# Chaining a kernel's small TensorE products into rows: probabilities times values, and S5's

## The chip, the cores and the metric

One NeuronCore of a Trainium2 chip runs the whole program. The metric is device time in microseconds (us), the median of the runs. TensorE (PE in the views) does the matrix products, with weights loaded beside them (PEld); VectorE (DVE) and ScalarE (ACT) work on tiles of 128 partitions; SyncE (SP) issues most transfers. Products write to PSUM, which has eight banks here.

## What is computed

Two layers of a decoder trunk on one sequence of 1024 tokens and 1024 channels, all in float32. Each layer is two residual steps:

```python
# h <- LayerNorm(alpha*h + Mixer(h));  h <- LayerNorm(alpha*h + ConvFFN(h))
# Mixer: ONE combined input projection whose columns are
#   [attn q | attn k | attn v | rg-lru x | rg-lru gate | s5 u]
#   - dilated sliding-window attention (6 heads of 64, rotary q/k)
#   - RG-LRU branch (causal conv4 -> gated linear recurrence, times a GeLU gate)
#   - S5: complex diagonal state space, 16 groups of 16 channels, 64 states -> GELU -> GLU
#   each output RMS-normalised, concatenated, ONE output projection
# ConvFFN: up-projection (2 x 3072) -> causal depthwise conv (width 3) -> GeLU-gated product -> down
scores = einsum('bnqchd,bnkchd->bnchqk', q, k) / 8      # masked by a dilated window, three dilations
out    = einsum('bnchqk,bnkchd->bnqchd', exp(scores - logsumexp(scores)), v)
```

## The kernel before, in words

Channels lie on partitions and tokens on columns for the projections. Every dense product is made of float32 values split in a high and a low part of a faster type (fp32r): three products of 128x512 columns for one of full precision. The span falls into stages: projections and S5 (to 115 us), attention of layer 0 (115 to 300), output projection (to 437), up-projection of the FFN (437 to 901), down-projection (to 1135); layer 1 the same again, with its S5 in 1176 to 1245, its attention in 1245 to 1440 and the end at 2302.

**Attention** (`attend`, L1164) goes by three pairs of heads (p) in a layer. `score(i, h)` (L1168) makes the scores of 128 queries (block i) of head h, takes their minimum with a custom VectorE operation (P, nb in the views), the exponential on ScalarE, a reciprocal and a scaling on VectorE. `apply(Q)` (L1194) takes two blocks of queries: for each block j of 128 keys it transposes the probabilities of both heads on TensorE (pt), copies them out of PSUM (PT; VectorE for even j, ScalarE for odd), and multiplies them with the values (o). `pv` (L1199) issues that product for one j, one step after its copy: two calls, one for each head, each with 64 columns of values, so each writes 64 of the 128 partitions of o. While a pair of blocks is scored, the blocks before it go through `apply`; `fill` (L1705) puts dense products of later work in between.

**S5** works by chunks of tokens. `states` (L931) multiplies inputs U with WvT, in calls that write 64 partitions (vps). `outputs` (L960) adds for each of eight groups of columns and each half b the product of U with TK (128x128) and two products of the states x with CA, whose 64 rows are the lower or upper half (by b); all of one b and one half h of the columns is summed in one bank (yps).

**The order.** The program is not issued as it is written. Every call of an engine is recorded (`Traced`, L437), a `Graph` (L195) gives each a duration (`estimate`, L274) and each handover from one engine to another a delay (HANDOVER, L185), and a planner (`make_plan`, L481) finds an order for all calls, and places in a pool of 46 tiles, eight half tiles and eight PSUM banks: `sweep` (L305) lists calls forward and backward in time, `improve` (L419) repeats it, and of five cycles the order that is shortest by the planner's own model is kept. `issue` (L145) emits it; each engine then runs its instructions in that order and waits on semaphores for the others. All recorded calls therefore carry line L149 in the views, and are told apart by the tile that they write. A product for one j or one q is one call to the planner, placed wherever it fits.

Of the kernel before, what the change touches and what calls it, by code (L numbers as in the profile page):

```python
# [40 lines left out]
RESP = 1  # L41
HOOKS = ((0, 1, "outputs_in"), (0, 7, "glu"))
# [75 lines left out]

class NoSlot(Exception):
# [3 lines left out]
class Planner:  # L123
# [36 lines left out]
    def scheduled(self, tc):  # L160
        return [self.position[i.name] for block in tc.compile_state.ordered_instructions_by_block.values()
                for i in block if i.name in self.position]

    def place(self, order):
        use = {}
        for t, c in enumerate(order):
            _, args, kwargs = self.calls[c]
            for a in (*args, *kwargs.values()):
# [26 lines left out]
class Graph:  # L195
# [7 lines left out]
    def __init__(self, planner):  # L203
# [7 lines left out]
        for c, (f, args, kwargs) in enumerate(calls):  # L211
            self.engine.append(ENGINES[str(f.__self__.engine).split(".")[-1]])
# [61 lines left out]
    def estimate(self, c, name, outs, ins):  # L274
        e = self.engine[c]
        n = size(outs[0].ap[1:])
        if e == "PE":
# [4 lines left out]
            elif outs[0].shape[0] == 64 and n > 127:  # L282
                t = n * 1.55 / 2.4
            else:
                t = (2 * n + 8) / 2.4
        elif e == "SP":
            t, self.bytes[c] = 60, size(outs[0].ap) * 4
        else:
            n = max([n] + [size(a.ap[1:]) for a in ins])
            if e == "ACT":  # L290
                t = 205 + 0.83 * n + (150 if n == 1024 and outs[0].dtype == F32 else 0)
            elif e == "POOL":
                t = 200 + n
            elif name == "scalar_tensor_tensor" and len(outs[0].ap) > 2 and n == 1024:
                t = 2125
            else:
                a, b = VECTOR.get(name, (145, 1.044))
                t = a + b * n
        self.time[c] = round(t)
# [137 lines left out]
class Traced:  # L437
# [5 lines left out]
    def __getattr__(self, name):  # L443
        f = getattr(self.engine, name)
        return lambda *args, **kwargs: self.calls.append((f, args, kwargs))

# [53 lines left out]
def emit(tc, A, out, planner, trace):  # L500
    nc = tc.nc
    V, ACT, POOL, PE, SP = (Traced(e, planner.calls) for e in (nc.vector, nc.scalar, nc.gpsimd, nc.tensor, nc.sync))
    with ExitStack() as ctx:
# [397 lines left out]
        class S5:  # L901
# [29 lines left out]
            def states(self):  # L931
# [886 lines left out]
```

## Time and profile before

| | |
|---|---|
| median of the runs | 2303.13 us |
| lowest | 2301.6 us |
| profiled execution | 2303.53 us |
| its span (first to last instruction) | 2301.7 us |
| TensorE matmul busy | 2242.8 us (97%) |
| weight loads busy | 1811.4 us (79%) |
| VectorE busy | 2045.1 us (89%) |
| ScalarE busy | 1154.0 us (50%) |
| chain that ended last | PE 84%, DVE 10%, ACT 3%, DMA 2%, issue 1% |

A busy time is the union of an engine's instruction times; matmuls are pipelined, so a record of 0.39 us of a product can be followed by the next after 0.23 us, and what an instruction costs is the distance from start to start. In a timeline, records of one kind that follow each other are drawn together, with their count; a float32 call leaves two records, an fp32r call one. PEclk is the TensorE clock granted, as a share of full speed.

### The profile page before, as it was taken

The numbers are of one execution on the slowest core, as the hardware profiler recorded it, in microseconds if no ns is written. First come the engines' busy times: TensorE is split into PE (matmuls) and PEld (weight loads), VectorE is DVE, ScalarE is ACT, GpSimd is POOL, SyncE is SP. The second block draws the span as 40 slices with busy tenths as digits, with TensorE's granted clock in tenths as the row PEclk, the third lists the DMA queues.
The fourth block names the chain that finished last, engine by engine and source line by source line (L and its number), as shares of the span: only waits on it lengthen the run. The fifth ranks groups of instructions, "written<-read, shape, count | busy, mean of one in ns | idle before, by whom it ended". The sixth has DMA issues, their size and how long they took to land.

```text
span 2301.7 us, 28256 instructions
## 1 busy us (share of the span) xinstructions
PE 2242.8 (97%) x10520; PEld 1811.4 (79%) x10520; DVE 2045.1 (89%) x3357; ACT 1154.0 (50%) x1773; POOL 4.0 (0%) x8
## 2 busy tenths in 40 slices
PE   8999999999999999999998899999999999999996
PEld 6867778878888888888886677788888888788884
DVE  8888878898888989999995877888899899899999
ACT  4275673754444445444735457727455444454441
POOL 0000000000000000000000000000000000000000
PEclk9999999999999999999999899999999999999998
DMA  5321150222233435322333521401222244363312
GB/s 208 87 80 44 33 174 29 83 83 83 92 110 138 158 108 201 110 99 103 128 101 94 180 74 42 147 36 75 91 84 99 92 155 156 108 215 111 120 69 83
DMA packets 82169, 246.38 MB, mean 107 GB/s; under 512 B 12464, under 2 KB 20784, under 8 KB 82032
## 3 DMA queue, kind: packets, MB, share of 16 engines
q1 hardware_dynamic: 82032, 244.59, 31.4%
q8 instruction: 82, 1.34, 0.2%
q14 instruction: 55, 0.45, 0.1%
HBM read 176.26 MB, written 60.82 MB: 103 GB/s over the span
## 4 chain that ended last, share of the span: by engine, by line
PE 84%; DVE 10%; ACT 3%; DMA 2%; issue 1%; DVEq 0%; ACTq 0%; SPq 0%
PE uP_n L149 34%; PE dP_n L149 17%; PE o_n L149 3%; PE s_n L149 2%; PE pt_n L149 2%; DVE yf_n L149 1%; PE yps_n L149 1%; DVE cg_n L149 1%; DMA wu_n<-in_w_up_dram 1%; DVE daP_n L149 1%; PE ups00c_n L149 1%; DVE dbP_n L149 1%; PE gtps01c_n L149 1%; PE vps_01c_n L149 1%; DVE cv_n L149 1%
## 5 line engine op out<-in xcount | busy, mean ns | idle before, releaser
L149 PE MATMUL dP_n<-dbP_n,daP_n 128*128 128x512 f32 x2016 | 462.2, 391 | 12.6 <-DVE yf_n L149 11.8
L149 PEld LDWEIGHTS dP_n<-dbP_n,daP_n 128*128 128x128 f32 x2016 | 379.6, 189 | 92.5 <-issue 12.5
L149 ACT ACTIVATE dbP_n<-wr_n 128x512 fp32r<-128x512 f32 x168 | 102.8, 627 | 104.7 <-DVE wr_n L149 49.7
L149 ACT ACTIVATE wA_n<-wu_n 128x512 fp32r<-128x512 f32 x144 | 89.9, 628 | 122.4 <-PE uP_n L149 41.9
L149 ACT ACTIVATE wS_n<-wu_n 128x512 fp32r<-128x512 f32 x144 | 90.2, 630 | 111.5 <-DVE wu_n L149 41.3
L149 ACT ACTIVATE daP_n<-gr_n 128x512 fp32r<-128x512 f32 x144 | 89.5, 628 | 112.8 <-PE dP_n L149 48.2
L149 DVE SCALAR_TENSOR_TENSOR cg_n<-ga_n,small,cg_n 128x1023 f32<-128x1023 f32 x96 | 122.9, 1280 | 23.4 <-ACT cg_n L149 22.6
L149 DVE SCALAR_TENSOR_TENSOR cv_n<-va_n,small,cv_n 128x1023 f32<-128x1023 f32 x96 | 122.8, 1280 | 16.2 <-ACT cv_n L149 16.0
L149 DVE TENSOR_TENSOR yf_n<-yf_n,dP_n 128x512 f32<-128x512 f32 x192 | 127.9, 689 | 4.4 <-PE dP_n L149 2.4
L149 DVE TENSOR_TENSOR dbP_n<-wr_n,dbP_n 128x512 fp32r<-128x512 f32 x168 | 116.0, 694 | 0.3 <-ACT dbP_n L149 0.3
L149 DVE TENSOR_TENSOR daP_n<-gr_n,daP_n 128x512 fp32r<-128x512 f32 x144 | 99.8, 694 | 2.4 <-ACT daP_n L149 2.4
L149 DVE TENSOR_TENSOR wS_n<-wu_n,wS_n 128x512 fp32r<-128x512 f32 x144 | 98.2, 687 | 3.3 <-ACT wS_n L149 2.8
L149 DVE TENSOR_TENSOR wA_n<-wu_n,wA_n 128x512 fp32r<-128x512 f32 x144 | 97.8, 687 | 3.1 <-ACT wA_n L149 2.9
L149 ACT ACTIVATE cg_n<-ga_n,small 128x1024 f32<-128x1024 f32 x48 | 59.7, 1243 | 73.9 <-DVE ga_n L149 51.2
L149 PE MATMUL pt_n<-ident,P_n 128*128 128x128 f32 x432 | 74.3, 285 | 11.2 <-DVE P_n L149 10.1
L149 PEld LDWEIGHTS pt_n<-ident,P_n 128*128 128x128 f32 x432 | 53.4, 144 | 33.7 <-DVE P_n L149 11.6
L149 DVE CUSTOM_DVE_ANT_0 P_n<-s_n,mask_n 128x512 f32<-128x512 f32 (+3 forms) x96 | 55.4, 586 | 22.6 <-PE s_n L149 21.9
L149 ACT ACTIVATE cv_n<-va_n,small 128x1024 f32<-128x1024 f32 x48 | 59.4, 1238 | 24.7 <-DVE va_n L149 18.5
L149 PE MATMUL o_n<-PT_n,vt_n 128*64 128x256 f32 (+1 forms) x480 | 71.1, 375 | 0.0
L149 DVE TENSOR_TENSOR uu_n<-uP_n,p_n 128x512 f32<-128x512 f32 x96 | 65.9, 687 | 3.7 <-PE uP_n L149 3.4
L149 PE MATMUL uP_n<-T1T4h_n,wA_n 128*128 128x512 f32 x192 | 64.0, 394 | 2.1 <-DVE uu_n L149 2.1
L149 PE MATMUL uP_n<-T0T3h_n,wS_n 128*128 128x512 f32 x192 | 63.4, 391 | 2.3 <-DVE uu_n L149 2.3
(2279 smaller groups left out, 5974.7 us busy)
## 6 DMA issues: line engine op xcount, KB each, us to landing
wu_n<-in_w_up_dram SPq DMA_DIRECT2D x96, 512.0 KB, 3.5
gd<-cg_n SPq DMA_DIRECT2D x48, 512.0 KB, 2.9
gr_n<-gd SPq DMA_DIRECT2D x48, 512.0 KB, 4.4
wr_n<-in_w_down_dram SPq DMA_DIRECT2D x48, 512.0 KB, 5.1
yr_n<-hres SPq DMA_DIRECT2D x24, 512.0 KB, 3.8
hres<-yr_n SPq DMA_DIRECT2D x24, 512.0 KB, 3.2
hres<-y_n SPq DMA_DIRECT2D x16, 512.0 KB, 2.6
yf_n<-hres SPq DMA_DIRECT2D x16, 512.0 KB, 5.2
```

The source lines that it names most:

```text
L149: i = f(*args, **kwargs)
```

## The change

A context `PE.row()` collects the matmul calls made inside it into one `Row`. To the planner a row is one call, with 350 (TURN, in ns) added to the sum of its calls' estimates; when it is issued, its calls follow each other, each bound to the one before by a dependency without a semaphore. The first is bound in that way to the twelve TensorE instructions ahead of it (BARRIER), and an instruction that follows within twelve is bound to the last of the row. Three places use rows: the products of probabilities and values, now collected over several key blocks (RUNS: after block 2; 4; 3 and 6; 4 and 8, by Q); S5.states (eight calls in a row); and S5.outputs, where TK's products are split in two halves of 64 columns and put in one row of 16 calls, and CA's 16 in a second. The planner's costs are changed as well.

```diff
+RUNS = ((2,), (4,), (3, 6), (4, 8))
...
     def issue(self, tc):
-        last = {}
-        for n in self.order:
-            f, args, kwargs = self.calls[n]
+        last, pe = {}, []
+        for n, (f, args, kwargs) in ((n, c) for n in self.order for c in parts(self.calls[n])):
             i = f(*args, **kwargs)
             i = getattr(i, "ins", i)
             self.position[i.name] = n
+            if i.engine == mybir.EngineType.PE:
+                row = n if isinstance(self.calls[n][0], Row) else None
+                pe.append((i.name, row))
+                if row is not None:
+                    after = pe[-2:-1] if pe[-2][1] == row else pe[-BARRIER:-1]
+                else:
+                    after = [x for x in pe[-BARRIER:-1] if x[1] is not None][-1:]
+                for x, _ in after:
+                    tc.add_manual_dep(i, x, mybir.DependencyInfo(mybir.DependencyClass.NoSync,
+                                                                 mybir.DependencyReason.DATA),
+                                      reason="a row's instructions follow each other")
...
+TURN = 350
+BARRIER = 12
-HANDOVER = {"PE": 230, "DVE": 90, "ACT": 120, "POOL": 100, "SP": 0}
-DMA_BYTES, DMA_DELAY = 380, 2000
-VECTOR = {"tensor_tensor": (145, 1.044), "scalar_tensor_tensor": (205, 1.05), "tensor_scalar": (180, 0.53),
-          "tensor_tensor_scan": (130, 2.1), "tensor_tensor_reduce": (250, 0.85)}
+HANDOVER = {"PE": 215, "DVE": 125, "ACT": 150, "POOL": 100, "SP": 0}
+DMA_BYTES, DMA_DELAY = 370, 2050
+VECTOR = {"scalar_tensor_tensor": (127, 1.044), "tensor_scalar": (95, 0.55), "tensor_tensor_scan": (47, 2.1),
+          "tensor_tensor_reduce": (165, 1.0)}
+OTHER = 66, 1.044
...
-            elif outs[0].shape[0] == 64 and n > 127:
-                t = n * 1.55 / 2.4
+            elif n == 1:
+                t = 109
             else:
-                t = (2 * n + 8) / 2.4
+                t = n * (8 if outs[0].shape[0] == ins[0].shape[0] == 128 else 4 if outs[0].shape[0] == 32 else 2) / 2.4
...
     # S5.states
                     for a in range(2):
-                        for q in range(4):
-                            gp = h * 4 + q
-                            for g2 in range(2):
-                                PE.matmul(vps[a][g2 * 64:(g2 + 1) * 64, q * 128:(q + 1) * 128],
+                        with PE.row():
+                            for q in range(4):
+                                gp = h * 4 + q
+                                for g2 in range(2):
+                                    PE.matmul(vps[a][g2 * 64:(g2 + 1) * 64, q * 128:(q + 1) * 128],
...
     # S5.outputs
-                    for q in range(4):
-                        gp = h * 4 + q
-                        c, d = slice(gp * 128, gp * 128 + 128), slice(q * 128, q * 128 + 128)
-                        for b in range(2):
-                            PE.matmul(yps[b][:, d], lhsT=T["TK"][b][:, c], rhs=U[b][:, c], start=True, stop=False)
-                        for a in range(2):
+                    at = [(slice(q * 128, q * 128 + 128), slice((h * 4 + q) * 128, (h * 4 + q) * 128 + 128))
+                          for q in range(4)]
+                    with PE.row():
+                        for d, c in at:
                             for b in range(2):
-                                p = slice(b * 64, b * 64 + 64)
-                                PE.matmul(yps[b][:, d][:, 1:], lhsT=T["CA"][a][p, c], rhs=self.x[a][p, c][:, :127],
-                                          start=False, stop=a == 1)
+                                for m in (slice(0, 64), slice(64, 128)):
+                                    PE.matmul(yps[b][m, d], lhsT=T["TK"][b][:, c][:, m], rhs=U[b][:, c],
+                                              start=d.start == 0, stop=False, skip_group_check=True)
+                    with PE.row():
+                        for d, c in at:
+                            for a in range(2):
+                                for b in range(2):
+                                    p = slice(b * 64, b * 64 + 64)
+                                    PE.matmul(yps[b][:, d][:, 1:], lhsT=T["CA"][a][p, c], rhs=self.x[a][p, c][:, :127],
+                                              start=False, stop=a == 1, skip_group_check=True)
...
     # apply(Q)
-                def pv(j, PT):
-                    lo = 1 if j == n - 1 else 0
-                    for h in range(2):
-                        PE.matmul(o[h * 64:h * 64 + 64, lo * 128:256],
-                                  lhsT=vt[:, j * 128 + h * 64:j * 128 + h * 64 + 64],
-                                  rhs=PT[:, h * 256 + lo * 128:h * 256 + 256], start=j == 0, stop=j == n - 1)
+                def pv():
+                    with PE.row():
+                        for j, PT in ready:
+                            lo = 1 if j == n - 1 else 0
+                            for h in range(2):
+                                PE.matmul(o[h * 64:h * 64 + 64, lo * 128:256],
+                                          lhsT=vt[:, j * 128 + h * 64:j * 128 + h * 64 + 64],
+                                          rhs=PT[:, h * 256 + lo * 128:h * 256 + 256], start=j == 0, stop=j == n - 1)
+                    ready.clear()
...
-                    if prev:
-                        pv(*prev)
-                    prev = (j, PT)
+                    ready.append((j, PT))
+                    if j + 1 in RUNS[Q]:
+                        pv()
                     yield
-                pv(*prev)
```

Since the costs and the calls change, the whole order is planned anew. In the pieces below a row is an instruction (x2 stands for two alike), with the line that issues it, what it writes and what it reads.

TensorE in S5.outputs of layer 0. Before, the products of one bank (yps000: layer 0, b = 0, h = 0) with TK (from U), with the first part of CA (from xr) and with the second (from xi) alternate:

```order
L149 MATMUL yps000_n123_226<-xi0_n91_190,ca01_n57_156 128x127
L149 MATMUL yps000_n123_226<-U00_n45_144,tk00_n80_179 128x128
L149 MATMUL yps000_n123_226<-xr0_n90_189,ca00_n56_155 128x127
L149 MATMUL yps000_n123_226<-xi0_n91_190,ca01_n57_156 128x127
L149 MATMUL yps000_n123_226<-U00_n45_144,tk00_n80_179 128x128
L149 MATMUL yps000_n123_226<-xr0_n90_189,ca00_n56_155 128x127
L149 MATMUL yps000_n123_226<-xi0_n91_190,ca01_n57_156 128x127
```

TensorE in the same part after (yps001 and yps011: b = 0 and b = 1 of the other half of the columns):

```order
L160 MATMUL yps011_n126_229<-U01_n46_145,tk01_n81_180 64x128 x2
L160 MATMUL yps001_n125_228<-U00_n45_144,tk00_n80_179 64x128 x2
L160 MATMUL yps011_n126_229<-U01_n46_145,tk01_n81_180 64x128 x2
L160 MATMUL yps001_n125_228<-xr0_n90_189,ca00_n56_155 128x127
L160 MATMUL yps011_n126_229<-xr0_n90_189,ca00_n56_155 128x127
L160 MATMUL yps001_n125_228<-xi0_n91_190,ca01_n57_156 128x127
L160 MATMUL yps011_n126_229<-xi0_n91_190,ca01_n57_156 128x127
```

TK's calls, now 64 partitions each, stand together, CA's behind them, with the two halves of the rows in turn.

TensorE at the last two query blocks of the first pair of heads in layer 1 (o103; s11... are scores of the next pair). Before:

```order
L149 MATMUL o103_n1676_1906<-PT1032_n1682_1912,vt10_n1511_1722 64x256 x2
L149 MATMUL s11010_n1713_1945<-k11a1_n1636_1861,q11a1_n1596_1815 128x256
L149 MATMUL s11010_n1713_1945<-k11a1_n1636_1861,q11b1_n1597_1816 128x256
L149 MATMUL o103_n1676_1906<-PT1033_n1686_1916,vt10_n1511_1722 64x256
L149 MATMUL s11100_n1715_1948<-k11a0_n1635_1860,q11a0_n1594_1813 128x256
L149 MATMUL s11100_n1715_1948<-k11a0_n1635_1860,q11b0_n1595_1814 128x256
L149 MATMUL o103_n1676_1906<-PT1033_n1686_1916,vt10_n1511_1722 64x256
L149 MATMUL o103_n1676_1906<-PT1034_n1688_1918,vt10_n1511_1722 64x256
```

TensorE at the same place after, ahead of the second of the two rows of o103:

```order
L160 MATMUL s11110_n1717_1951<-k11a1_n1636_1861,q11a1_n1596_1815 128x256
L160 MATMUL s11110_n1717_1951<-k11a1_n1636_1861,q11b1_n1597_1816 128x256
L160 MATMUL s11200_n1719_1954<-k11a0_n1635_1860,q11a0_n1594_1813 128x384
L160 MATMUL s11200_n1719_1954<-k11a0_n1635_1860,q11b0_n1595_1814 128x384
L160 MATMUL q12pc0_n1712_1943<-ln20t0h00_n1424_1620,q12wh_n1710_1941 128x512
L160 MATMUL q12pc0_n1712_1943<-ln20t0l00_n1425_1621,q12wh_n1710_1941 128x512
L160 MATMUL s11510_n1760_2002<-k11a1_n1636_1861,q11a1_n1596_1815 128x512
L160 MATMUL s11510_n1760_2002<-k11a1_n1636_1861,q11b1_n1597_1816 128x512
L160 MATMUL o103_n1676_1906<-PT1034_n1688_1918,vt10_n1511_1722 64x256 x2
L160 MATMUL o103_n1676_1906<-PT1035_n1690_1920,vt10_n1511_1722 64x256 x2
L160 MATMUL o103_n1676_1906<-PT1036_n1692_1922,vt10_n1511_1722 64x256 x2
L160 MATMUL o103_n1676_1906<-PT1037_n1694_1924,vt10_n1511_1722 64x128 x2
```

The two heads' calls, which scores came between, stand side by side, and four key blocks are one run; six more score products stand ahead of this piece, behind the last transposes.

TensorE at the start of layer 1's attention (k11pc: the dense products that give the keys of the second pair; s10...: the first scores). Before, and then after:

```order
L149 MATMUL k11pc1_n1622_1845<-ln20t4h31_n1463_1667,k11wh_n1600_1819 128x512
L149 MATMUL k11pc1_n1622_1845<-ln20t4l31_n1464_1668,k11wh_n1600_1819 128x512
L149 MATMUL k11pc1_n1622_1845<-ln20t4h31_n1463_1667,k11wl_n1601_1820 128x512
L149 MATMUL s10000_n1562_1774<-k10a0_n1558_1769,q10a0_n1547_1758 128x256
L149 MATMUL s10000_n1562_1774<-k10a0_n1558_1769,q10b0_n1548_1759 128x256
```

```order
L160 MATMUL s10210_n1592_1811<-k10a1_n1559_1770,q10a1_n1549_1760 128x384
L160 MATMUL s10210_n1592_1811<-k10a1_n1559_1770,q10b1_n1550_1761 128x384
L160 MATMUL k11pc0_n1602_1821<-ln20t0l10_n1427_1623,k11wh_n1600_1819 128x512
L160 MATMUL k11pc0_n1602_1821<-ln20t0h10_n1426_1622,k11wl_n1601_1820 128x512
L160 MATMUL k11pc0_n1602_1821<-ln20t0h10_n1426_1622,k11wh_n1600_1819 128x512
L160 MATMUL k11pc0_n1602_1821<-ln20t0l10_n1427_1623,k11wh_n1600_1819 128x512
```

The keys' products, all ahead of the first score before, stand among the scores after. VectorE among the scores of the same pair of heads (yr: the residual's operations; P, nb: a score block), before and after:

```order
L149 TENSOR_TENSOR yr17_n1704_1934<-yr17_n1704_1934,lg01_n1695_1925 128x1024
L149 TENSOR_SCALAR P1041_n1626_1849<-P1041_n1626_1849,nb__1041_1850 128x640
L149 RECIPROCAL nb__1050_1856<-nb__1050_1856 128x1
L149 TENSOR_TENSOR yr10_n1697_1927<-yr10_n1697_1927,lg01_n1695_1925 128x1024
L149 TENSOR_SCALAR P1050_n1631_1855<-P1050_n1631_1855,nb__1050_1856 128x768
```

```order
L160 TENSOR_SCALAR P1041_n1626_1849<-P1041_n1626_1849,nb__1041_1850 128x640
L160 ISA P1051_n1639_1864,nb__1051_1865<-s10511_n1641_1867,mask1_n1497_1708,nb__1051_1865 128x256
L160 ISA nb__1051_1865 128x1
L160 RECIPROCAL rs51_1681<-rs51_1681 128x8
L160 ISA P1060_n1650_1876,nb__1060_1877<-s10600_n1651_1878,mask1_n1497_1708 128x512
```

Two of the yr operations that stood between scalings are no longer there.

## Rows read from the trace of the kernel before

**Rows 1.** The page, busy time of each engine: us, share of the span, instructions.

```profile
PE 2242.8 (97%) x10520; PEld 1811.4 (79%) x10520; DVE 2045.1 (89%) x3357; ACT 1154.0 (50%) x1773; POOL 4.0 (0%) x8
```

**Rows 2.** Windows by stage: us; busy PE, PEld, DVE, ACT, POOL; clock, DMA share, GB/s.

```profile
31.40:115.10 83.70, 81.66 (x458) 66.40 (x457) 73.47 (x193) 22.08 (x32) 0.00 (x0) 1.00 0.30 79
115.10:300.00 184.90, 179.77 (x986) 134.14 (x985) 153.31 (x331) 116.12 (x206) 0.00 (x0) 0.98 0.22 64
436.70:901.00 464.30, 461.41 (x2036) 379.28 (x2035) 418.77 (x563) 231.85 (x329) 1.92 (x2) 1.00 0.33 114
1176.40:1244.90 68.50, 68.50 (x378) 55.89 (x377) 40.56 (x53) 18.43 (x23) 0.00 (x0) 1.00 0.28 74
1244.90:1440.00 195.10, 180.39 (x942) 133.47 (x940) 163.18 (x339) 114.77 (x203) 0.00 (x0) 0.95 0.30 97
```

**Rows 3.** Timeline of TensorE, attention of layer 0: start, us, instruction, shapes, count.

```profile
160.77 0.65 PE L149 MATMUL o_n<-PT_n,vt_n 128*64 128x256 f32 x2
161.35 0.33 PE L149 MATMUL pt_n<-ident,P_n 128*128 128x128 f32 x1
161.61 0.65 PE L149 MATMUL o_n<-PT_n,vt_n 128*64 128x256 f32 x4
162.19 0.33 PE L149 MATMUL pt_n<-ident,P_n 128*128 128x128 f32 x1
...
165.68 1.73 PE L149 MATMUL pt_n<-ident,P_n 128*128 128x128 f32 x13
```

**Rows 4.** The same timeline, a run of sixteen records between dense products.

```profile
169.11 0.40 PE L149 MATMUL q02pc_n<-xTl_n,q02wh_n 128*128 128x512 f32 x1
169.44 1.95 PE L149 MATMUL o_n<-PT_n,vt_n 128*64 128x256 f32 x16
171.32 0.50 PE L149 MATMUL q02pc_n<-xTh_n,q02wl_n 128*128 128x512 f32 x1
171.65 0.39 PE L149 MATMUL q02pc_n<-xTh_n,q02wh_n 128*128 128x512 f32 x1
171.88 0.40 PE L149 MATMUL q02pc_n<-xTl_n,q02wh_n 128*128 128x512 f32 x1
```

**Rows 5.** Timeline of TensorE, S5's outputs of layer 0.

```profile
96.61 0.49 PE L149 MATMUL yps_n<-U_n,tk_n 128*128 128x128 f32 x2
97.03 0.48 PE L149 MATMUL yps_n<-xr_n,ca_n 64*128 64x127 f32 x2
...
97.67 0.49 PE L149 MATMUL yps_n<-U_n,tk_n 128*128 128x128 f32 x2
...
102.53 0.37 PE L149 MATMUL yps_n<-xr_n,ca_n 64*128 64x127 f32 x1
102.54 0.37 PE L149 MATMUL yps_n<-xi_n,ca_n 64*128 64x127 f32 x1
102.74 0.27 PE L149 MATMUL yps_n<-xr_n,ca_n 64*128 64x127 f32 x1
```

**Rows 6.** Timeline of TensorE, S5.states of layer 1.

```profile
1179.46 1.09 PE L149 MATMUL vps_n<-U_n,WvT_n 128*64 128x128 f32 x16
1180.49 0.66 PE L149 MATMUL vtp_n<-ident,vr_n 128*128 128x128 f32 x4
```

**Rows 7.** Windows at the starts of the two attention stages, columns as in rows 2.

```profile
1244.90:1300.00 55.10, 41.26 (x179) 31.47 (x178) 50.43 (x107) 30.67 (x54) 0.00 (x0) 0.81 0.34 111
115.00:135.00 20.00, 14.92 (x79) 11.35 (x78) 17.92 (x45) 16.90 (x32) 0.00 (x0) 0.92 0.51 127
```

**Rows 8.** Waits of TensorE, 1244.9 to 1300: us in total, times, longest.

```profile
PE pt_n L149 <- DVE P_n L149: 8.4, 4, 4.9
...
PE s_n L149 <- DVE PT_n L149: 0.8, 1, 0.8
```

**Rows 9.** VectorE by form, 1244.9 to 1300: busy us, mean ns, idle before.

```profile
L149 DVE TENSOR_TENSOR yr_n<-yr_n,lg_n 128x1024 f32<-128x1024 f32 x4 | 4.8, 1208 | 0.0
L149 DVE COPY PT_n<-pt_n 128x512 f32<-128x512 f32 x6 | 4.1, 683 | 0.0
```

More of the change, by code (lines that the diff above doesn't have):

```diff
@@ L2 @@
 import math
-from contextlib import ExitStack
+from contextlib import ExitStack, contextmanager
 import numpy as np
@@ L116, in layout, with __init__, parts @@
     return {k: np.ascontiguousarray(v, dtype=f) for k, v in arrays.items()}
+class Row:
+    def __init__(self, calls):
+        self.calls = calls
+def parts(call):
+    return call[0].calls if isinstance(call[0], Row) else [call]
 class NoSlot(Exception):
@@ L160, in scheduled @@
     def scheduled(self, tc):
-        return [self.position[i.name] for block in tc.compile_state.ordered_instructions_by_block.values()
-                for i in block if i.name in self.position]
+        last = {}
+        for block in tc.compile_state.ordered_instructions_by_block.values():
+            for i in block:
+                if i.name in self.position:
+                    n = self.position[i.name]
+                    last.pop(n, None)
+                    last[n] = i
+        return list(last)
     def place(self, order):
@@ L166, in place @@
         for t, c in enumerate(order):
-            _, args, kwargs = self.calls[c]
-            for a in (*args, *kwargs.values()):
+            for a in (a for _, args, kwargs in parts(self.calls[c]) for a in (*args, *kwargs.values())):
                 n = self.tile_of(a)
@@ L210, in __init__ @@
         seen = {}
-        for c, (f, args, kwargs) in enumerate(calls):
-            self.engine.append(ENGINES[str(f.__self__.engine).split(".")[-1]])
+        for c, (f, args, kwargs) in ((c, x) for c, call in enumerate(calls) for x in parts(call)):
+            if c == len(self.engine):
+                self.engine.append(ENGINES[str(f.__self__.engine).split(".")[-1]])
+                self.time[c] = TURN * isinstance(calls[c][0], Row)
             kw = dict(kwargs)
@@ L290, in estimate @@
             if e == "ACT":
-                t = 205 + 0.83 * n + (150 if n == 1024 and outs[0].dtype == F32 else 0)
+                t = 75 + 0.87 * n + 115 * (len(outs) > 1) + 150 * (n == 1024 and outs[0].dtype == F32) + 140 * (n == 256)
             elif e == "POOL":
@@ L294, in estimate @@
             elif name == "scalar_tensor_tensor" and len(outs[0].ap) > 2 and n == 1024:
-                t = 2125
+                t = 2050
             else:
-                a, b = VECTOR.get(name, (145, 1.044))
+                a, b = VECTOR.get(name, OTHER)
                 t = a + b * n
-        self.time[c] = round(t)
+        self.time[c] += round(t)
     def lag(self, a, b):
@@ L445, in __getattr__, with row @@
         return lambda *args, **kwargs: self.calls.append((f, args, kwargs))
+    @contextmanager
+    def row(self):
+        n = len(self.calls)
+        yield
+        self.calls[n:] = [(Row(self.calls[n:]), (), {})]
 class Slots:
@@ L938, in states @@
                     for a in range(2):
-                        for q in range(4):
-                            gp = h * 4 + q
-                            for g2 in range(2):
-                                PE.matmul(vps[a][g2 * 64:(g2 + 1) * 64, q * 128:(q + 1) * 128],
-                                          lhsT=T["WvT"][a][:, gp * 128 + g2 * 64:gp * 128 + g2 * 64 + 64],
-                                          rhs=U[g2][:, gp * 128:gp * 128 + 128], start=True, stop=True)
+                        with PE.row():
[3 more added lines that the diff above has]
+                                    PE.matmul(vps[a][g2 * 64:(g2 + 1) * 64, q * 128:(q + 1) * 128],
+                                              lhsT=T["WvT"][a][:, gp * 128 + g2 * 64:gp * 128 + g2 * 64 + 64],
+                                              rhs=U[g2][:, gp * 128:gp * 128 + 128], start=True, stop=True)
                     mul(vr[:, hv], vps[0], er[:, hv])
@@ L1196, in apply @@
                 n = 2 * Q + 2
[L1197 to L1204 removed]
+                ready = []
+                def pv():
[7 more added lines that the diff above has]
+                    ready.clear()
                 for j in range(n):
```

1 line of the change is left out of this document (removed).

## The prediction

> **What bounds the kernel now.** I read the page's first part, then the windows by stage, then the instructions of TensorE one by one. The page gives TensorE 2242.8 us of matmul time in a span of 2301.7, VectorE 2045.1 and ScalarE 1154.0 [rows 1]: TensorE has work nearly all the time, VectorE nine tenths of it. By stage, TensorE is idle for 2.0 us of 83.7 in the first projections with S5, 2.9 us of 464.3 in the up-projection, none in the S5 stretch of layer 1; it idles in the two attention stages, 5.1 and 14.7 us [rows 2]. So everywhere else the span moves with what TensorE's instructions occupy, and the change is priced by their distance from start to start. Transfers are no bound: the DMA engines are busy for 0.33 of a stage at most [rows 2].
>
> That distance depends on what stands next to what. Dense products of 512 columns start 0.23 us apart (171.65, 171.88) [rows 4]; of transposes of 128x128, 13 last 1.73 us and one alone 0.33, so they are (1.73 - 0.33) / 12 = 0.117 apart [rows 3]. Products of probabilities and values write 64 partitions each; the calls of heads 0 and 1 run side by side in the two halves of TensorE's columns. One call leaves two records in this view, so x4 is one pair of calls, x16 four pairs. A run of one pair lasts 0.58 us from its start to the next start, a run of four pairs 1.88 [rows 3, 4]: 0.433 a pair, and 0.15 for the run, however long it is. The neighbours pay too. The dense product ahead of the run of 16 is followed after 0.33 us rather than 0.23, and so is the one behind it [rows 4]; a transpose between two runs takes 0.26 rather than 0.117 [rows 3]. So one run in another shape costs 0.15 + 0.10 + 0.10 = 0.35 us between dense products, 0.15 + 0.14 = 0.29 between transposes; I take 0.33. A call that stands alone (x2 at 160.77) also lasts 0.58: it costs as much as a pair and wastes half of it, 0.215 us.
>
> **Products of probabilities and values.** 240 calls before and after: 96 pairs of 256 columns, 24 pairs of 128. The emitted order of before has them in 85 runs, 26 of them with an odd number of calls; that of after has 36, all in pairs (6 of two pairs' length, 12 of three, 18 of four). Working: 96 x 0.433 + 24 x 0.217 = 46.8 for the pairs on either side; before adds 26 x 0.215 = 5.6 and 85 x 0.33 = 28.1, after 36 x 0.33 = 11.9. Saved: 5.6 + 28.1 - 11.9 = **21.8 us**. The bounds of the turn, 0.29 and 0.35, give 19.8 and 22.8.
>
> **S5's outputs.** Before, one product with TK (128x128) and two with CA (64 rows) alternate; the cycle is 97.67 - 96.61 = 1.06 us, of which TK takes 0.42 and the two CA 0.64 [rows 5]. There are 32 such cycles in both layers: 33.9 us. After, TK's 32 products are 64 half-column calls, in pairs like the run of vps below, which writes 128 columns in two halves: 8 calls (x16) last 1.03 us [rows 6], that is 0.15 and four pairs at 0.22. So 32 x 0.22 = 7.0. The CA products of b = 0 and b = 1 sit in different halves of the rows and alternate. The trace has one such place: two CA products of different halves start at 102.53 and 102.54, the next at 102.74 [rows 5], so a pair costs 0.21. I take 32 x 0.22 = 7.0, the other end being 64 x 0.22 = 14.1 if the halves ran one behind the other. The order has 9 runs for all of this (5 and 4); 9 x 0.35 = 3.2. Saved: 33.9 - 7.0 - 7.0 - 3.2 = **16.7 us**, at least 9.6. Half of it, 8.3, is layer 1's, in the stretch with no idle TensorE time; the other half layer 0's, in the first stage with 2.0 us of it [rows 2].
>
> S5.states gains nothing: the order has 6 runs of vps before and 5 after, kps 3 and 4.
>
> **Waits that a row adds.** A row is one call to the planner, so it waits for its last copy of transposed probabilities, and everything behind it on TensorE waits with it; before, a call waited for its own copy only. The copy takes 0.683 us on VectorE and can stand behind an operation of 1.208 us [rows 9], so a row set right behind its transposes would stall up to 0.683 + 1.208 = 1.9 us. But the order puts work between: ahead of the second o103 row stand twelve score products and two dense ones (the pieces shown), more than 2 us; ahead of other rows there are 8 to 20 instructions. TensorE's waits in the worst stretch are 8.4 us for P and 0.8 for a copy [rows 8]. I cost this at nothing; its upper end is a rival below.
>
> **The new order of everything.** The costs change, so the plan is another one. The products of the dense stages are the same in number; what their order can gain there is bounded by the idle time [rows 2]. The two starts of the attention stages are the place where it matters. Layer 1's first 55.1 us have 41.26 of TensorE work, VectorE busy for 50.43, a clock of 0.81; 20 us of layer 0's start have 14.92 and 0.92 [rows 7]. A mean of 0.81 is made of time at 2.4 and at 1.2 GHz, the lower level behind idle time. VectorE sets the pace there: TensorE waits for P. After puts two things differently. First, 41 products of k11 and 33 of k01 (by the order), which before stood ahead of the first score, stand behind it as filler for idle TensorE time: 41 x 0.23 = 9.4 us and 33 x 0.23 = 7.6, the latter at most the 5.1 us idle. Second, on VectorE, between the first score's operation and the last scaling of pair 0 in layer 1, six yr operations become two and wv11l is gone: wv11l is of the same size, so 5 x 1.208 = 6.0 us less [rows 9]. At most 9.4 + 6.0 + 5.1 = 20.5; at least nothing, since idle time that is filled here may open elsewhere while VectorE keeps its own sum (163 of 195 us in this stage). I take a little over half, 8 for layer 1 and 4 for layer 0: **12 us**.
>
> Sum on the profiled execution: 2301.7 - 21.8 - 16.7 - 12 = 2251.2, plus 1.8 outside its span (2303.53 - 2301.7) = **2253 us**. The profiled execution is 0.4 us above the median, which I leave.
>
> **Rivals.**
>
> R1, *the starts don't recover*: the turns are saved, but the attention stages stay on VectorE's pace, 153.31 and 163.18 us of work that the change doesn't lessen [rows 2]. Time: 2253 + 12 = 2265. For it: VectorE is 92% busy in layer 1's start [rows 7]. Against: at 83% over each whole stage it has room. The Trainium skill, TensorEngine Tiling (Array Packing), section PSUM Bottleneck, says that packing speeds TensorE and not the copying out of PSUM, which may become the bottleneck. By that rule the starts give nothing and R1's time holds; this trace agrees in the start (8.4 us waiting for P) and not over the stage.
>
> R2, *the starts recover in full*: 20.5 instead of 12 gives 2244, and with the idle time of the up-projection (2.9) on top 2242.
>
> R3, *S5 gives half*: the CA products of the two halves run one behind the other (9.6 instead of 16.7), or layer 1's stretch isn't bound by the time that matmuls hold; either gives 2260 to 2261. For the second: the stretch's weight loads fill 55.89 of 68.5 us (82%), as in the up-projection, 379.28 of 464.3 [rows 2]. Against: the gap shown is between starts, 0.32 a CA product where 0.11 would do. The Trainium skill, Trainium Kernel Development and Optimization, section Performance Expectations, calls busy time of matmuls a bad metric of how near the limit a kernel is, and that of weight loads a good one. By that rule S5's stretch has no more to give than the dense ones; the starts in the rows speak otherwise.
>
> R4, the other side: *rows wait for their last copy*. 36 rows; the turns saved are 38.5 us, so from 38.5 / 36 = 1.07 us a row the change loses. At 1.5, between that and the 1.9 above, 36 x 1.5 = 54: 2301.7 - 38.5 + 54 + 1.8 = 2319, without the starts' gain. For it: VectorE is 83% busy, so a copy often finds it taken. Against: the work that stands between, and that ScalarE makes every second copy and is busy 60% of the stage.
>
> That the rows don't form is no rival: they stand in the emitted order.
>
> **How the numbers follow.** A measurement of this kernel tells some 2%, 46 us, from no change: faster means under 2257. Forecast (2246 to 2261) 0.46; R1 (2260 to 2273) 0.22; R2 0.15; R3 0.06; R4 0.11. Under 2257: two thirds of the forecast (0.32), all of R2 (0.15), a little of R1 and R3 (0.05), together 0.52; over 2349, R4 at over 2.3 us a row, 0.03; the rest, 0.45, lies between. The range takes R2 with some of layer 0's gain beyond its bound, 2232, and R1 with a few rows waiting, 2280; what is left out is most of R4 and the tails, near 2 in 10. The likeliest case's own range is 2246 to 2261.
>
> **What would show it.** Right: runs of o as 8, 12 or 16 records with one turn each, distances 0.43 a pair; TK's records at 0.22 a pair, CA's two halves starting within 0.02 us; the stretch of S5 in layer 1 about 8 us shorter than 68.5; layer 1's first attention stage some 20 us shorter than 195.1 (half of 21.8 turns, 8 at the start), with idle time under 8. Wrong: CA records 0.22 apart one by one (R3); the start's idle time as before (R1); waits of o for PT in the view of waits, many of them over 1 us (R4); or a stage outside attention and S5 that moves by more than 5 us, which none of my terms holds.

## The result, and the profile after

The changed kernel takes 2250.82 us (median of 4, 2248.82 to 2253.55) where the one before takes 2303.13 (median of three; a fourth run of it took 5909.03 us and is left out): a ratio of 0.9774, 95% interval 0.9754 to 0.9793. The forecast was 2253 us, and faster. The profiled execution has a span of 2247.0 us, 54.7 less than the 2301.7 of before. First the page's row on the engines, which answers to [rows 1]:

```profile
PE 2196.0 (98%) x10584; PEld 1796.6 (80%) x10584; DVE 2043.2 (91%) x3357; ACT 1154.9 (51%) x1775; POOL 4.0 (0%) x8
```

TensorE is busy for 46.8 us less, VectorE's and ScalarE's work is what it was. Where the 54.7 us came from is seen in windows between the same six events of either kernel: first product of V in layer 0, first score, first product of the output projection, the next layer's first product, its first score, its output projection, the end. After:

```profile
core 0: us, PE busy (x) PEld busy (x) DVE busy (x) ACT busy (x) POOL busy (x), PEclk, DMA share, GB/s
33.30:109.80 76.50, 69.22 (x457) 55.87 (x456) 72.76 (x194) 22.32 (x31) 0.00 (x0) 0.96 0.37 104
109.80:328.40 218.60, 214.74 (x1210) 170.13 (x1209) 183.97 (x363) 150.01 (x246) 0.00 (x0) 1.00 0.23 72
328.40:1122.50 794.10, 791.85 (x3533) 653.44 (x3532) 731.77 (x1073) 398.19 (x600) 1.91 (x2) 1.00 0.32 112
1122.50:1215.90 93.40, 90.10 (x577) 74.66 (x575) 83.93 (x151) 47.16 (x70) 0.00 (x0) 1.00 0.52 159
1215.90:1436.30 220.40, 217.86 (x1222) 172.75 (x1223) 194.92 (x370) 143.00 (x240) 0.00 (x0) 1.00 0.28 92
1436.30:2247.00 810.70, 786.83 (x3497) 649.81 (x3495) 751.72 (x1093) 374.39 (x566) 0.00 (x0) 0.99 0.31 110
```

The same windows of before, where they aren't those of [rows 2] (its first row is the first here too):

```profile
115.10:339.50 224.40, 219.27 (x1178) 164.06 (x1177) 180.85 (x359) 147.30 (x245) 0.00 (x0) 0.98 0.26 78
339.50:1135.30 795.80, 791.28 (x3533) 652.12 (x3532) 734.59 (x1080) 395.34 (x594) 1.92 (x2) 1.00 0.31 109
1135.30:1244.90 109.60, 109.08 (x588) 88.46 (x587) 80.25 (x141) 47.04 (x71) 0.00 (x0) 1.00 0.37 111
1244.90:1487.10 242.20, 226.60 (x1176) 169.40 (x1175) 199.45 (x376) 147.09 (x245) 0.00 (x0) 0.96 0.30 100
1487.10:2301.70 814.60, 790.13 (x3502) 651.05 (x3500) 751.73 (x1090) 374.33 (x563) 0.00 (x0) 0.99 0.31 109
```

Layer 0, from V to the output projection: 83.7 + 224.4 = 308.1 before, 295.1 after, 13.0 less. Layer 1, over the same parts: 351.8 and 313.8, 38.0 less. The projections and FFNs: 1.7 and 3.9 less. What lies ahead of V took 1.9 more, but from execution to execution of one and the same order that start moves between 30.8 and 33.3 us. Together 54.7. So layer 1 gave three times what layer 0 gave, which the prediction had at 27.2 and 23.2.

The rows in the timeline of TensorE (start, us, instruction, shapes, count), one of probabilities and values, then one of TK and the beginning of one of CA in layer 1:

```profile
162.22 1.95 PE L160 MATMUL o_n<-PT_n,vt_n 128*64 128x256 f32 x16
164.10 0.66 PE L160 MATMUL pt_n<-ident,P_n 128*128 128x128 f32 x4
...
1192.74 1.97 PE L160 MATMUL yps_n<-U_n,tk_n 128*64 128x128 f32 x32
1194.64 0.49 PE L160 MATMUL yps_n<-xr_n,ca_n 64*128 64x127 f32 x4
1194.96 0.39 PE L160 MATMUL yps_n<-xi_n,ca_n 64*128 64x127 f32 x4
1195.18 0.39 PE L160 MATMUL yps_n<-xr_n,ca_n 64*128 64x127 f32 x4
```

Four pairs take 1.88 us as in [rows 4]; TK's 16 calls take 1.90; of CA, two calls (x4 is two records each) take 0.22, so the halves of the rows do run side by side. The waits of TensorE in the whole execution, longest first:

```profile
PE dP_n L160 <- DVE yf_n L160: 11.6, 2, 9.4
PE q01pc_n L160 <- DVE q01wl_n L160: 7.3, 1, 7.3
PE ups00c_n L160 <- ACT wu00h_n L160: 7.2, 1, 7.2
PE s_n L160 <- DVE k10a_n L160: 2.6, 1, 2.6
PE pt_n L160 <- DVE P_n L160: 2.3, 3, 0.9
```

Of the 8.4 us of waiting for P in layer 1's start [rows 8] 0.7 are left. No row of o waits for a copy; the waits for a copy (PT) that there are belong to scores and transposes, 2.5 us in two places (1.6 before). New is a wait of 7.3 us for q01wl, in layer 0's S5.

### The profile page after: what moved, and what is told of

Same layout as the page of the kernel before. It is cut to its first block, busy times and chain, and to the rows that moved or that the text cites. A ratio compares the mean times of both kernels' runs of the same rounds, so it can differ in the third digit from the quotient of the medians.

```text
span 2247.0 us, 28432 instructions
## 1 busy us (share of the span) xinstructions
PE 2196.0 (98%) x10584; PEld 1796.6 (80%) x10584; DVE 2043.2 (91%) x3357; ACT 1154.9 (51%) x1775; POOL 4.0 (0%) x8
## 4 chain that ended last, share of the span: by engine, by line
PE 85%; DVE 10%; ACT 2%; DMA 1%; issue 1%; SPq 0%; DVEq 0%; ACTq 0%
PE uP_n L160 37%; PE dP_n L160 18%; PE o_n L160 2%; PE s_n L160 2%; PE pt_n L160 2%; DVE yf_n L160 1%; DVE P_n L160 1%; PE ht_n L160 1%; PE ups00c_n L160 1%; DVE cg_n L160 1%; DVE e_n L160 1%; DVE v_n L160 1%; DVE wv_n L160 1%; PE vps_12c_n L160 1%; PE gtps10c_n L160 1%
## 5 line engine op out<-in xcount | busy, mean ns | idle before, releaser
L160 PE MATMUL dP_n<-dbP_n,daP_n 128*128 128x512 f32 x2016 | 463.2, 391 | 12.7 <-DVE yf_n L160 11.6
L160 DVE SCALAR_TENSOR_TENSOR cv_n<-va_n,small,cv_n 128x1023 f32<-128x1023 f32 (+1 forms) x96 | 122.3, 1280 | 6.8 <-ACT cv_n L160 6.5
L160 DVE CUSTOM_DVE_ANT_0 P_n<-s_n,mask_n 128x512 f32<-128x512 f32 (+3 forms) x96 | 55.4, 587 | 23.2 <-PE s_n L160 21.8
L160 PE MATMUL uP_n<-T1B11h_n,wA_n 128*128 128x512 f32 x192 | 65.2, 392 | 0.0
L160 PE MATMUL uP_n<-T0B11h_n,wA_n 128*128 128x512 f32 x192 | 64.4, 392 | 0.0
```

## The experiments

Nine of the twelve kernels keep the changed kernel's order: the list of calls and the places of the tiles that its planner chose are written into the file, so that an edit moves only what it names. Three (costs_only, rows_oldcosts and long_new) are planned anew.

### What one turn costs: dose_mid and dose_end

Transposes that nobody reads, between the pairs of a row or behind them.

```diff
# dose_mid, inside the loop over a row's key blocks
+if j != ready[-1][0]:
+    PE.matmul(o[:, 256:384], lhsT=PT[:, :128], rhs=ident, start=False, stop=False,
+              is_transpose=True, skip_group_check=True)
# dose_end, behind that loop
+for _, PT in ready[:-1]:
+    PE.matmul(o[:, 256:384], lhsT=PT[:, :128], rhs=ident, start=False, stop=False,
+              is_transpose=True, skip_group_check=True)
```

> The changed kernel in its own order, with one 128x128 transpose, whose result nobody reads, between any two pairs of calls inside a row of probabilities and values: 84 transposes, and 84 more runs. If a turn costs what I worked out between transposes: 84 x (0.117 + 0.29) = 34.2 us, so 2250.8 + 34 = 2285. If turns are hidden or much cheaper: 84 x 0.117 = 9.8, 2261. If a turn costs 0.35: 2290.

> The same 84 transposes, all at the end of their row: no run more. Both theories: 84 x 0.117 = 9.8 us, so 2261; what it has less than the kernel with the transposes inside is the price of 84 turns, 24 us by the one theory, near 0 by the other.

Measured: 2280.7 us (2279.47 to 2281.86) and 2256.08 (2254.20 to 2257.37). The two kernels hold the same instructions; 84 turns lie between them (271 changes of tile shape in the trace against 103) and 24.6 us, so a turn costs **0.293 us of the whole kernel's time**, or 0.27 to 0.32 by the spread of the runs. Worked out ahead of it were 0.29 between transposes. The same row as above, in dose_mid:

```profile
163.75 0.65 PE L163 MATMUL o_n<-PT_n,vt_n 128*64 128x256 f32 x4
164.34 0.33 PE L163 MATMUL o_n<-ident,PT_n 128*128 128x128 f32 x1
164.60 0.65 PE L163 MATMUL o_n<-PT_n,vt_n 128*64 128x256 f32 x4
...
166.28 0.65 PE L163 MATMUL o_n<-PT_n,vt_n 128*64 128x256 f32 x4
166.87 0.66 PE L163 MATMUL pt_n<-ident,P_n 128*128 128x128 f32 x4
```

3.12 us instead of 1.88, for three transposes: 0.41 each, of which 0.117 is its own. The transposes themselves came cheaper than forecast: dose_end is 5.3 us over the changed kernel, not 9.8. What took up the rest wasn't looked into.

### The order without the rows, the rows without the order: costs_only and rows_oldcosts

```diff
# costs_only
-HANDOVER = {"PE": 230, "DVE": 90, "ACT": 120, "POOL": 100, "SP": 0}
-DMA_BYTES, DMA_DELAY = 380, 2000
+HANDOVER = {"PE": 215, "DVE": 125, "ACT": 150, "POOL": 100, "SP": 0}
+DMA_BYTES, DMA_DELAY = 370, 2050
...
# rows_oldcosts
-HANDOVER = {"PE": 215, "DVE": 125, "ACT": 150, "POOL": 100, "SP": 0}
-DMA_BYTES, DMA_DELAY = 370, 2050
+HANDOVER = {"PE": 230, "DVE": 90, "ACT": 120, "POOL": 100, "SP": 0}
+DMA_BYTES, DMA_DELAY = 380, 2000
...
```

The first is the kernel before with all planner's costs of the changed one (VECTOR and the estimates too), the second the changed kernel with those of before.

> The kernel before with the planner's new costs and no rows. If the turns between tile shapes are the gain, this kernel has none of it: its order has 281 changes of tile shape (247 before, 103 after), so 17 more runs at 0.33 us, +5.6 us, and its attention starts may gain up to the 12 us that I gave them, since 48 products of k11 and 24 of k01 stand behind the first scores: 2297, between 2285 and 2310. If the new order is the gain, it is at most 2265. In layer 1's attention start: if filler products are what fills it, TensorE's idle time there falls from 13.8 us to under 6; if it is S5's outputs coming early that frees VectorE (here they end only 13 products ahead of the first score, 55 after), idle stays over 8 us.

> The changed kernel with the planner's costs of before: rows, 93 changes of tile shape. If the turns are the gain: 2303 - 38.5 and up to 12 for the starts, 2253 to 2266. If the new costs' order is the gain: 2290 or more.

Measured, with the kernel before at 2302.84 beside them: costs_only 2281.0 (ratio 0.9907, 0.9892 to 0.9922), rows_oldcosts 2244.74 (0.9751, 0.9736 to 0.9765). The rows bring 58 us with the old costs. The costs bring 22 us without rows (under 2% of the time, but well clear of the spread of the runs), in spite of 17 runs more (5 to 6 us): below my 2285 to 2310, and far above the other theory's 2265. With rows, the new costs bring nothing; by the medians they lose 6, though the intervals of the two ratios overlap. So rows and costs don't add up: each leads to a new plan, and each new plan fills layer 1's start. The windows below run from layer 1's first score to the end of the 16th scaling of P, which is the whole first pair of heads; in the order before, after, costs_only, rows_oldcosts (columns as above):

```profile
1244.90:1305.60 60.70, 46.65 (x217) 34.91 (x215) 53.72 (x113) 32.92 (x58) 0.00 (x0) 0.83 0.34 111
```

```profile
1215.90:1266.70 50.80, 48.26 (x264) 37.63 (x264) 47.08 (x106) 34.25 (x61) 0.00 (x0) 1.00 0.33 104
```

```profile
1231.00:1285.20 54.20, 54.20 (x286) 42.67 (x284) 49.17 (x106) 37.56 (x65) 0.00 (x0) 1.00 0.31 97
```

```profile
1211.80:1268.10 56.30, 54.07 (x295) 42.41 (x296) 52.76 (x112) 37.59 (x64) 0.00 (x0) 1.00 0.39 127
```

In all three new plans TensorE gets through 47 to 78 instructions more, in 4 to 10 us less, at a clock of 1.00 instead of 0.83. Of those instructions 113, 139 and 135 are dense products, where before has 73: more filler in every new plan. VectorE's work in the window falls by 6.6, 4.6 and, in rows_oldcosts, only 1.0 us. In costs_only, TensorE has no idle time at all, though S5's outputs end just ahead of the first score: that they come early is not what frees the start, and by the test set in my expectation this speaks for the filler.

### What filled the start: k11_first and yr14_late

Moved in the list of calls: 19 products of k11pc0 from among the first scores to ahead of s10000, or two VectorE operations from ahead of s10000 to among the scores.

```diff
# k11_first
+PE matmul k11pc0,k11wl,ln20t0h00
+PE matmul k11pc0,k11wh,ln20t0h10
...
 PE matmul s10000,q10a0,k10a0
...
-PE matmul k11pc0,k11wl,ln20t0h00
-PE matmul k11pc0,k11wh,ln20t0h10
...
# yr14_late
-DVE tensor_tensor yr14,yr14,lg01
-DVE tensor_tensor yr14,yr14,lb01
...
 DVE tensor_tensor_reduce P1020,s10200,mask1
+DVE tensor_tensor yr14,yr14,lg01
...
+DVE tensor_tensor yr14,yr14,lb01
```

> The changed kernel in its own order, with the 19 products of k11pc0 that stand among layer 1's first scores put ahead of the first score (4.4 us of TensorE work that can no longer fill idle time). If filling is what recovered the start: up to 4.4 us longer, 2253 to 2255, and TensorE's idle time from the first score to the output projection rises from 5.1 by 2 to 4.4. If the start recovered since S5's outputs come earlier and VectorE has less to do there: under 1 us, 2251.

> The changed kernel in its own order, with the two operations of yr14 (1.2 us each) on VectorE moved from ahead of layer 1's first score into its first scores. If VectorE sets the pace there: up to 2.4 us longer, 2252 to 2253.5; if TensorE's filler covers it: 2251.

k11_first took 2251.04 us, no more than the changed kernel. In its trace, the window to the 16th scaling:

```profile
1216.50:1268.10 51.60, 46.48 (x247) 35.60 (x246) 47.62 (x105) 33.92 (x60) 0.00 (x0) 0.97 0.33 101
1216.50:1437.80 221.30, 216.08 (x1205) 170.73 (x1205) 195.49 (x370) 142.62 (x238) 0.00 (x0) 0.99 0.28 91
```

17 instructions fewer than after, and 0.8 us longer. The second row, from the first score to the output projection, has 5.2 us of idle TensorE time where after has 2.5. But the wait of 2.6 us for k10a just ahead of the first score, in the list of waits above, is gone: the products that were moved fill it. My 5.1 us had counted both, and both together are what they were (5.1 and 5.2). So the run moved filler from one gap to another and lost nothing by it; it does not show that the start can do without filler, of which 97 dense products are left in the window. yr14_late took 2250.85, but tells nothing of its question: the framework's own scheduler orders the emitted calls again for each engine, and the program that came out has VectorE's two operations where they were, 24.9 and 23.7 us ahead of the first score. It stands as a repeat of the changed kernel: 2250.85 for 2250.82. (k11_first's move did come through, in 17 of the 19.)

The other candidate is VectorE's sum in the window. Length beside VectorE's busy time in the five windows shown: 60.7 and 53.7, 56.3 and 52.8, 54.2 and 49.2, 51.6 and 47.6, 50.8 and 47.1. They fall together, as they should where VectorE sets the length; the share that is yr is 8.4 us before (7 operations) and 2.4 after (2). That it is these operations is argued from the sums and not shown, since the one run for it didn't move them. And they are not what the new plans share: rows_oldcosts has five yr operations in the window and 1.0 us less VectorE work than before, and yet TensorE is idle there for 2.2 us instead of 14.1. What all of them share is the filler. That it alone fills the start is likely by this and not shown: no run takes all of it out.

### The wait for q01wl in layer 0: q01_only, q01wl_early and bind64

TensorE at that place in the changed kernel, and VectorE beside it:

```profile
76.88 0.44 PE L160 MATMUL yps_n<-U_n,tk_n 128*64 128x128 f32 x4
84.60 0.79 PE L160 MATMUL q01pc_n<-xTh_n,q01wl_n 128*128 128x512 f32 x1 [7.28 <-DVE q01wl_n L160]
85.19 0.63 PE L160 MATMUL q01pc_n<-xTh_n,q01wh_n 128*128 128x512 f32 x1
85.62 0.63 PE L160 MATMUL q01pc_n<-xTl_n,q01wh_n 128*128 128x512 f32 x1
...
88.31 1.88 PE L160 MATMUL yps_n<-U_n,tk_n 128*64 128x128 f32 x28
```

```profile
78.28 5.15 DVE L160 TENSOR_TENSOR_SCAN v_n<-r,v_n 128x128 f32<-128x128 f32 x16
83.34 1.20 DVE L160 TENSOR_TENSOR q01wl_n<-q01wr_n,q01wh_n 128x1024 fp32r<-128x1024 f32 x1
```

The new plan puts q01wl behind 16 scans. And the row is broken: its first two calls stand ahead of eight products of q01pc, the first of which needs q01wl; the plan had them behind the row, more than 12 instructions away, where no binding reaches. Behind the idle time dense products start 0.43 us apart for a while, not 0.23: the lower of the clock's two levels.

```diff
# q01_only and q01wl_early, list of calls
+DVE tensor_tensor q01wl,q01wr,q01wh
 DVE tensor_tensor_scan v00,r8,v00
...
 DVE tensor_tensor_scan v01,r8,v01
-DVE tensor_tensor q01wl,q01wr,q01wh
# q01wl_early and bind64
-BARRIER = 12
+BARRIER = 64
```

> The changed kernel in its own order, with only q01wl made ahead of the 16 scans of layer 0's S5, rows bound to 12 instructions as in the changed kernel (so no new order ahead of the row). The wait of 7.3 us goes. If it was lost time: 2242. If S5's chain paces the stretch: TensorE gets to the first row of CA some 8 us early and waits there for xi, made at about 92 or 93; 2248 to 2250, with about 6 us of idle time before 110.

> The changed kernel in its own order, but VectorE makes q01wl ahead of the 16 scans of layer 0's S5 rather than behind them, and a row is bound to 64 instructions on either side rather than 12, so that the first row of TK stays whole. In the changed kernel TensorE waits 7.3 us for q01wl at 77 and then runs eight products at half the clock. If that wait is simply lost time: 7.3 + 8 x 0.2 + 0.3 = 9 us less, 2242. If VectorE's chain of S5 (scans, v, xr, xi) paces this stretch, the wait moves to the row of CA, which needs xi (made by 91.8 in the changed kernel, 1.2 later here; the row starts at 95.3): at most 2 us less, 2249.

> The changed kernel in its own order with rows bound to 64 instructions on either side, VectorE's order as it is: the first row of TK stays whole, one run less. If the broken row is what costs: 2242. If q01wl being late is: the wait stands behind the row, 5.5 instead of 7.3 us, 2248.5 to 2251.

Measured: 2251.99, 2251.41 and 2251.47, all what the changed kernel takes. The waits of TensorE from 30 to 125 us, of q01_only and then of q01wl_early (bind64 has 4.2 us for q01wl, where I had 5.5, 3.7 for vr and 1.2 for TK's transfer):

```profile
PE q01pc_n L163 <- DVE q01wl_n L163: 2.2, 1, 2.2
PE vtp_n L163 <- ACT vr_n L163: 1.8, 1, 1.8
PE s_n L163 <- DVE nb__0000_213 L163: 1.6, 1, 1.6
PE yps_n L163 <- DVE xi_n L163: 0.8, 1, 0.8
```

```profile
PE vtp_n L163 <- ACT vr_n L163: 5.0, 1, 5.0
PE yps_n L163 <- DMA tk_n<-ksb_n: 2.0, 1, 2.0
PE yps_n L163 <- DVE xi_n L163: 1.6, 1, 1.6
```

The wait goes to whatever is late next: vr, TK's own transfer, xi, the first scores. In q01_only the first score comes 1.6 us sooner after V than in the changed kernel, and at the output projection the lead is down to 0.2. The place named in my expectation, CA's row waiting for xi, holds only 0.8 and 1.6 us of it; that VectorE's S5 chain alone paces the stretch is not what these waits say. What they show is that the 7.3 us at q01wl are not time that can be had back by making q01wl early. From V to the output projection TensorE is idle for 11.1 us in the changed kernel and for 10.0, 11.6 and 12.1 in q01_only, q01wl_early and bind64; before, it was 7.2.

### S5's rows: ca_serial and tk_whole

```diff
# ca_serial
-for d, c in at:
-    for a in range(2):
-        for b in range(2):
+for b in range(2):
+    for d, c in at:
+        for a in range(2):
# tk_whole
-for m in (slice(0, 64), slice(64, 128)):
-    PE.matmul(yps[b][m, d], lhsT=T["TK"][b][:, c][:, m], rhs=U[b][:, c],
-              start=d.start == 0, stop=False, skip_group_check=True)
+PE.matmul(yps[b][:, d], lhsT=T["TK"][b][:, c], rhs=U[b][:, c],
+          start=d.start == 0, stop=False, skip_group_check=True)
```

> The changed kernel in its own order; inside a row of CA products those of the lower half of the rows all stand ahead of those of the upper half instead of in turn. If the halves ran side by side only because they take turns: a row takes 16 x 0.22 + 0.15 = 3.7 instead of 1.98 us, four rows 6.8 more, 2254 to 2258 (layer 0's two may be hidden). If the halves' order doesn't matter: 2251.

> The changed kernel in its own order, with TK's products as calls of 128x128 as before, 8 in a row, instead of pairs of half-column calls. If the 0.42 us that such a call took in the kernel before is its own time: 8 x 0.42 = 3.4 instead of 1.9 us a row, four rows 5.9 more less four turns, 2252 to 2256. If it was 0.22 and the turn from CA and back: 32 x 0.22 = 7.0, as the halves, and fewer turns, 2249 to 2250.

ca_serial took 2255.3 us, 4.5 over the changed kernel. Its CA calls come one by one, 0.22 us for a call where after has two:

```profile
1197.16 0.48 PE L163 MATMUL yps_n<-xr_n,ca_n 64*128 64x127 f32 x2
1197.49 0.38 PE L163 MATMUL yps_n<-xi_n,ca_n 64*128 64x127 f32 x2
1197.71 0.38 PE L163 MATMUL yps_n<-xr_n,ca_n 64*128 64x127 f32 x2
```

A row takes 3.43 us (1197.16 to 1200.59) instead of 1.98, four rows 5.8. (Calls in turn also write to different banks, that of b = 0 and that of b = 1; the run doesn't tell the two apart.) tk_whole took 2252.01, and its row of TK

```profile
1194.89 1.95 PE L163 MATMUL yps_n<-U_n,tk_n 128*128 128x128 f32 x16
1196.76 0.49 PE L163 MATMUL yps_n<-xr_n,ca_n 64*128 64x127 f32 x4
```

1.87 us for eight whole calls, where 16 half ones take 1.90. The 0.42 of [rows 5] was 0.22 and a turn. Splitting TK gains nothing; putting its calls together does.

### Longer rows: long_new

```diff
-RUNS = ((2,), (4,), (3, 6), (4, 8))
+RUNS = ((2,), (4,), (6,), (8,))
```

> The changed kernel planned anew with one row for all key blocks of a pair of query blocks (2, 4, 6, 8): 24 rows instead of 36, 72 changes of tile shape instead of 103, and in its order q01wl is made early. If only turns count: 12 x 0.33 = 4.0 less, 2247; if the plan has no wait like that for q01wl on top, 2240 to 2244. If rows now wait for their last copy (half tiles: eight in all, and the longest row takes all eight): 2251 or more, with TensorE waiting for PT.

2240.5 us (2239.36 to 2242.76; ratio to before 0.9730, 0.9716 to 0.9745), 10.3 less than the changed kernel and the fastest of all: 24 rows of o, 72 changes of tile shape. Its rows wait for a copy twice in the execution, 0.5 us together; the eight half tiles are enough. The twelve turns would be 3.5 (at 0.293) to 4.0 us of the 10.3; the rest I put down to another plan, as with the 6 us between old and new costs, but no run holds the order fixed there.

## Why the prediction held, step by step

**The turns** (21.8 us for probabilities and values): right, in kind and size. Summing each run of o from its first start to the next instruction of another shape gives 65.2 us in 85 runs before and 52.1 in 36 after; with the 0.18 us that each run costs its neighbours, 80.5 and 58.6, so 21.9. Of that 13.1 are read from the traces and the rest is worked out; at the dose's 0.293, within my 0.29 to 0.35, the 49 turns and the 5.6 for odd calls make 20.0. The order showed 36 rows, and they ran as 36.

**S5's outputs** (16.7): right in size, one price misread. Layer 1's four rows run from 1192.74 to 1200.50, 7.8 us, where I had 17.2 / 2 = 8.6; before, its 16 cycles took 16.7 (1214.31 to 1222.65 and 1230.26 to 1238.60), where I had 17.0: 8.9 saved. Layer 0's went from 15.5 to 8.1, idle time left out, 7.4 saved; one cycle of 1.06 stood for all, and there they were shorter. Together 16.3. The halves of CA overlap, and ca_serial shows that it is the turn-taking that makes them. TK's 0.42 held a turn, so the half columns that I priced at 0.22 were no gain in themselves (tk_whole). But the step "the other half layer 0's, in the first stage with 2.0 us of it" failed: that window of layer 0 now has 7.3 us of idle time and eight products at the lower clock, and one of its four rows ran in two parts. By order of VectorE's instructions, q01wl behind the scans could have been seen.

**Waits that a row adds**, at nothing: right. No row of o waits for a copy, and in long_new, with rows up to eight blocks, for 0.5 us. R4 is out.

**The starts** (12, at most 20.5): the step that was mis-sized. Layer 1 gave 38.0; less 8.9 for S5 and 11.0 for turns, 18.1 is its start's, where I had 8 and a bound of 15.4. The bound left out the clock. In the window of the 16th scaling TensorE's idle time fell from 14.1 us to 2.5, which is 11.5 (10.3 over the whole layer). And 217 instructions took 46.65 busy us where at the pace of after (48.26 / 264 = 0.183) they take 39.7: 6.9 us that idle time alone doesn't count. The two stretches of that window in which the lower clock was granted, before, columns as above, say the same:

```profile
1261.60:1275.30 13.70, 8.62 (x33) 7.24 (x34) 11.78 (x24) 7.82 (x11) 0.00 (x0) 0.50 0.43 129
1288.90:1295.70 6.80, 5.13 (x13) 3.36 (x14) 6.77 (x15) 2.86 (x5) 0.00 (x0) 0.50 0.39 140
```

13.75 busy us at half the clock are 6.9 at the full one. Idle time and clock, 10.3 + 6.9, make 17.2 of the 18.1. Of my two mechanisms, the filler stands in every plan that fills this start and VectorE's shorter list doesn't (rows_oldcosts); neither was tested by itself. The rows aren't needed for it: the new costs' plan alone fills that start to the last. Layer 0 gave 13.0 where I had 23.2. Turns are 11.0 + 7.4 = 18.4 of it, but idle time, which my 4 us for the start should have lowered, rose by 4.0: from 2.0 us to 7.3 in the first stage, and from 5.1 to only 3.9 in attention. Its start did recover (TensorE is busy for 19.23 of its first 20 us, from 109.8, and for 14.92 before [rows 7], the clock 1.00); the idle time came up elsewhere, at q01wl above all. The last 1.4 us stay open; eight products at the lower clock are in them.

So the sum is right to 2 us by luck: two errors of some 10 us went in opposite directions, layer 1's start larger, layer 0's gain smaller. **R1** would have been 2265: out. **R2**, the starts in full, was right for layer 1, which went beyond it, and wrong for layer 0. **R3** out on both counts: layer 1's S5 outputs went from 16.7 to 7.8 us. The Trainium skill's rule for weight loads (Trainium Kernel Development and Optimization, Performance Expectations), read as in R3, would have left that stretch as long as before; the weight loads' share of the span moved from 79 to 80%. The Trainium skill's rule on copying out of PSUM (TensorEngine Tiling (Array Packing), PSUM Bottleneck) didn't bind here: VectorE went from 89 to 91% and no copy held a row up.

Not settled: why the plan made with old costs and no rows, and it alone of the plans seen, left layer 1's start so empty; how much of that start is filler and how much VectorE's shorter list; and what in layer 0 would have to move for its S5 to keep the 8 us.

## What to carry to other kernels

Small products that use part of TensorE pay by the run, not by the call: count the changes of shape in the emitted order and multiply by what two runs of different length show, and the saving of grouping them is known before it runs. Idle time at a start cost more than itself here, since products behind it ran at the lower clock (11.5 us of idle time and 6.9 of clock): take both. Where a planner makes the order, a change of its costs or calls is a new plan, and plans differ by 6 to 22 us here for no reason that the change states: compare the edit at a fixed order, and treat one plan's wait as movable until an experiment shows that it goes away and the end with it.

## What the runs showed of the hardware that was not expected

A 128x128 float32 product of 128 columns in a row of its kind takes 0.23 us (1.87 for eight), as long as two half-column calls side by side (1.90 for eight pairs). Two 64-row calls overlap only where they alternate between the halves of the rows (here also between two banks): 0.22 us a pair in turn, 0.22 us a call one behind the other.
